# A two-layer hybrid decoder trunk: tiles at multiples of 256 bytes, and layer 1's values and gates projected 512 columns at a time

## The chip, the cores and the metric

The kernel runs on one core of a Trainium2 chip. The metric is the device time of one execution in microseconds (us); the time given for a kernel is the median of its runs. The engines are named as the profile names them: PE is the tensor engine, which multiplies a stationary operand (loaded as "weights", PEld) with a moving one; DVE the vector engine, ACT the scalar engine, POOL the third elementwise engine, SP the engine that issues the DMAs. SBUF is the on-chip memory that operands are read from, PSUM the one that matmuls write to.

## What is computed

Two residual layers on x (512 tokens by 1024 features, float32) and a final norm:

```python
def even_layer(x, g_norm, w_in, b_f, w_out):          # layer 0
    z = rms_norm(x, g_norm) @ w_in                    # q, k, v, gate of 16 + 16 heads of 64, forget gates
    ya = forgetting_attention(hA(qa), hA(ka), hA(va), log_f)   # causal softmax, cumulative log-forget bias
    yb = dilated_attention(hB(qb), hB(kb), hB(vb))             # causal softmax over dilated windows
    return x + concat(ya * silu(ga), yb * silu(gb)) @ w_out

def odd_layer(x, g_norm, w_in, w_out):                # layer 1
    q, k, v, g = split(rms_norm(x, g_norm) @ w_in)    # 4 heads: q, k 256 wide, v, g 512 wide
    y = retention(rotate(q), rotate(k) / 16, v)       # o_t = sum_{s<=t} gamma^(t-s) (q_t.k_s) v_s
    return x + (head_group_norm(y) * silu(g)) @ w_out

out = rms_norm(odd_layer(even_layer(x)), final_norm)
```

## The kernel before

All matmuls of the layers run on `float32r` operands. To keep float32 accuracy, every operand is held as a high and a low part (`split`, L130 to L136: ACT writes the high part, DVE subtracts it for the low part), and a product is three matmuls into the same PSUM tile: high x high, high x low, low x high (`three`, L185 to L188). Thus one line of the page stands for a third of a product.

The normed x is kept transposed in `xT` (128 features of a block, high and low, 8 blocks, 512 tokens). The weights come as a stream of 512 KB chunks: `load_next` issues the DMA of the next chunk of the `plan` into one of three `w_raw` buffers, `split_next` makes its parts `w_h` and `w_l` in one of three buffers each (512 elements of a row at a time, so two ACT and two DVE instructions per chunk) and loads the next; `weights` is called by whoever needs a chunk, so one chunk is split for each one taken.

Three helpers use them. `proj_features` (PSUM tile `pf`) has a chunk of 512 rows by 256 columns as the stationary operand and 512 tokens of `xT` as the moving one: 96 matmuls of 512 columns for 256 features. `proj_tokens` (`pt`) has 128 tokens of `xT` as the stationary operand and 256 columns of a chunk as the moving one: 96 matmuls of 256 columns for 256 features and 512 tokens; two token tiles share a PSUM tile, and the two chunks are used one after the other, each for all four token tiles. `out_proj` (`po`) moves 512 columns of a chunk of 256 rows. PSUM tiles of these three come from one pool of three buffers (`pp`).

Layer 0 works through eight groups of four heads. The projections of the next group and the output projection of an earlier one are fillers, put between the attention steps of a group by `interleave`: logits `ps_s`, softmax on DVE, ACT and POOL, the transposes `ps_pt`, and `ps_o`, probabilities by values. Layer 1 works through four heads in the same way: scores `ps_a` (`kh`, `kl` stationary, `qh`, `ql` moving, 512, 384, 256 and 128 columns wide), retention `ps_r` (`vh`, `vl` moving, 512 wide), group norm on DVE, the gate on POOL, the transposes `ps_yt`. The fillers there are the output projection of the head before and the projections of the next head: `qk`, then the gate (`g_done` copies PSUM to SBUF on DVE; after the last copy ACT applies silu), then the values (`v_done` splits them). Within an engine, instructions run in the order in which the build has put them; an engine that waits holds up all that stands behind.

Tiles are laid out one behind the other in the order in which pools and tiles are made, and small ones take at least 32 bytes of a row. Where they begin in the built program, as the remainder by 256 bytes: `xT` at 128, the weight buffers at 160, layer 0's large tiles (`q`, `k`, `v`, probabilities, `yh`, `yl`) at 64, layer 1's (`kh`, `qh`, `vh`, `ah`, `y1h` and their low parts) and the one extra weight buffer of the last output projection at 32.

## Time and profile before

| | before |
|---|---|
| median of 3 runs | 1035.87 us (1035.27 to 1036.48) |
| span of the profiled execution | 1035.3 us |
| PE busy | 1002.6 us, 97%, 5836 matmuls |
| weight loads (PEld) busy | 869.6 us, 84% |
| DVE busy | 637.0 us, 62% |
| ACT busy | 472.4 us, 46% |
| POOL busy | 247.4 us, 24% |
| HBM read over the span | 85.39 MB, together with writes 85 GB/s |

The profile is one execution, traced on the chip. Busy time counts an instruction from its start to its end; the matmuls of PE are pipelined and overlap, so the busy share says that PE always had one in work, not how fast they follow each other. For that the timeline is read: the distance between the starts of neighbouring matmuls. The chain of work that ended last runs over PE for 81% of the span, over DVE for 7%, DMA for 5% and ACT for 4%.

### The profile page before, as it was taken

Reading aid. Unit: us, or ns where it says so; the run is one execution under the profiler, and the core shown is the slowest. Engines: PE = TensorE matmul, PEld = TensorE weight load, DVE = VectorE, ACT = ScalarE, POOL = GpSimd, SP = SyncE. Lnnn points to the kernel's source line nnn. Section 1 sums busy time; section 2 is a strip of 40 time slices with the busy share of each in tenths; the row PEclk is TensorE's granted clock in tenths of the full one; section 3 lists DMA queues with packets and bytes.
Section 4 is the critical chain, followed back from the end, with each engine's and each line's share of the span. In section 5 each row is a group of like instructions: output and inputs, shape, how many; then the busy total and the mean of one; then the engine's idle time right before and its main releaser. Section 6 shows DMA issues by size and latency. Waiting matters only on the chain.

```text
span 1035.3 us, 15756 instructions
## 1 busy us (share of the span) xinstructions
PE 1002.6 (97%) x5836; PEld 869.6 (84%) x5836; DVE 637.0 (62%) x1389; ACT 472.4 (46%) x987; POOL 247.4 (24%) x326
## 2 busy tenths in 40 slices
PE   5999999999999999999999989999999999999997
PEld 5879788888887888987887769978998899889975
DVE  6465676575584576675657684377645744674476
ACT  5345464464554545644657473333323232333233
POOL 3011354454354352211212140023100300030012
PEclk8999999999999999999999999999999999999999
DMA  7554878635647776437454125321222222312112
GB/s 211 133 134 90 150 100 103 177 77 120 156 90 108 143 84 139 107 79 145 76 130 123 41 62 184 102 79 64 82 82 91 72 82 82 102 61 95 69 41 82
DMA packets 84444, 107.42 MB, mean 104 GB/s; under 512 B 6016, under 2 KB 63616, under 8 KB 84240
## 3 DMA queue, kind: packets, MB, share of 16 engines
q1 hardware_dynamic: 84368, 106.42, 43.4%
q8 instruction: 46, 0.75, 0.3%
q14 instruction: 30, 0.25, 0.1%
HBM read 85.39 MB, written 2.13 MB: 85 GB/s over the span
## 4 chain that ended last, share of the span: by engine, by line
PE 81%; DVE 7%; DMA 5%; ACT 4%; issue 2%; POOL 1%; SPq 0%; DVEq 0%; POOLq 0%; ACTq 0%
PE pf L186 10%; PE pf L187 10%; PE pf L188 10%; PE pt L186 8%; PE pt L188 8%; PE pt L187 8%; PE po L186 5%; PE po L188 5%; PE po L187 5%; PE ps_pt L457 3%; DMA kb<-ka 2%; PE ps_o L470 2%; DVE w_l L134 2%; PE ps_o L469 2%; PE ps_s L443 1%
## 5 line engine op out<-in xcount | busy, mean ns | idle before, releaser
L134 DVE TENSOR_TENSOR w_l<-w_raw,w_h 128x512 fp32r<-128x512 f32 x288 | 218.3, 785 | 95.0 <-ACT w_h L132 81.7
L132 ACT ACTIVATE w_h<-w_raw 128x512 fp32r<-128x512 f32 x288 | 169.5, 627 | 186.0 <-PE pf L187 60.2
L186 PE MATMUL pt<-w_h,xT 128*128 128x256 f32 x768 | 217.1, 283 | 2.2 <-ACT xT L132 2.1
L188 PE MATMUL pt<-w_h,xT 128*128 128x256 f32 x768 | 215.7, 281 | 1.6 <-DVE xT L134 1.6
L187 PE MATMUL pt<-w_l,xT 128*128 128x256 f32 x768 | 215.5, 281 | 0.0
L186 PE MATMUL pf<-xT,w_h 128*128 128x512 f32 x512 | 204.4, 399 | 0.0
L188 PE MATMUL pf<-xT,w_l 128*128 128x512 f32 x512 | 202.9, 396 | 0.0
L187 PE MATMUL pf<-xT,w_h 128*128 128x512 f32 x512 | 202.9, 396 | 0.0
L450 POOL TENSOR_SCALAR pi<-pi,st 128x512 f32<-128x512 f32 (+3 forms) x128 | 73.5, 575 | 377.2 <-DVE st L449 346.6
L186 PEld LDWEIGHTS pt<-w_h,xT 128*128 128x128 f32 x768 | 145.3, 189 | 3.7 <-ACT xT L132 2.9
L188 PEld LDWEIGHTS pt<-w_h,xT 128*128 128x128 f32 x768 | 145.2, 189 | 1.8 <-DVE xT L134 1.8
L187 PEld LDWEIGHTS pt<-w_l,xT 128*128 128x128 f32 x768 | 145.2, 189 | 1.1 <-DVE w_l L134 0.2
L188 PEld LDWEIGHTS pf<-xT,w_l 128*128 128x128 f32 x512 | 96.5, 188 | 23.2
L186 PEld LDWEIGHTS pf<-xT,w_h 128*128 128x128 f32 x512 | 96.7, 189 | 19.9
L187 PEld LDWEIGHTS pf<-xT,w_h 128*128 128x128 f32 x512 | 96.7, 189 | 19.6
L132 ACT ACTIVATE pth<-ps_pt 128x512 fp32r<-128x512 f32 (+3 forms) x128 | 55.3, 432 | 98.2 <-PE ps_pt L457 85.7
L448 ACT ACTIVATE pi<-pi,st 128x512 f32<-128x512 f32 (+3 forms) x128 | 71.4, 558 | 44.4 <-DVE st L446 43.8
L704 POOL TENSOR_TENSOR yn<-yn,gate 128x512 f32<-128x512 f32 x16 | 21.9, 1367 | 262.8 <-DVE yn L703 249.4
L253 DVE TENSOR_TENSOR xres<-po,xres 128x512 f32<-128x512 f32 x88 | 59.6, 683 | 26.6 <-PE po L188 26.1
L134 DVE TENSOR_TENSOR ptl<-ps_pt,pth 128x512 fp32r<-128x512 f32 (+3 forms) x128 | 62.2, 487 | 21.2 <-ACT pth L132 19.4
L457 PE MATMUL ps_pt<-ident,pi 128*128 128x128 f32 x320 | 56.8, 275 | 0.1
L446 DVE CUSTOM_DVE_ANT_0 pi<-ps_s,bias 128x512 f32<-128x512 f32 (+1 forms) x64 | 30.8, 487 | 40.6 <-PE ps_pt L457 20.6
(155 smaller groups left out, 1614.1 us busy)
## 6 DMA issues: line engine op xcount, KB each, us to landing
w_raw<-in_even_w_in_dram SPq DMA_DIRECT2D x64, 512.0 KB, 5.6
w_raw<-in_odd_w_in_dram SPq DMA_DIRECT2D x48, 512.0 KB, 3.5
w_raw<-in_even_w_out_dram SPq DMA_DIRECT2D x16, 512.0 KB, 4.3
w_raw<-in_odd_w_out_dram SPq DMA_DIRECT2D x16, 512.0 KB, 3.5
qb<-qa SPq DMA_DIRECT2D x32, 128.0 KB, 2.9
qb<-qa SPq DMA_DIRECT2D x16, 256.0 KB, 3.2
qa<-qa SPq DMA_DIRECT2D x32, 128.0 KB, 3.1
cs<-c_dram SPq DMA_DIRECT2D x16, 256.0 KB, 3.6
```

The lines of the kernel that those rows point to most:

```text
L132: act.activation(hi, src, AF.Copy, scale=scale)
L134: dve.tensor_tensor(lo, src, r32(hi), ALU.subtract)
L186: pe.matmul(ps, lhsT=ah, rhs=bh, start=first, stop=False)
L187: pe.matmul(ps, lhsT=ah, rhs=bl, start=False, stop=False)
L188: pe.matmul(ps, lhsT=al, rhs=bh, start=False, stop=last)
L253: dve.tensor_tensor(xr, ps, xr, ALU.add)
L446: dve.tensor_tensor_reduce(pi[:, 0:n], ps[:, 0:n], hs["bias"](i), 1.0, 3e38, ALU.add, ALU.min, st[:, 0:1])
L448: act.activation(pi[:, 0:n], pi[:, 0:n], AF.Exp, bias=st[:, 0:1], scale=-1.0, accum_out=st[:, 1:2])
L450: pool.tensor_scalar(pi[:, 0:n], pi[:, 0:n], st[:, 2:3], 1.0, ALU.mult, ALU.mult)
L457: pe.transpose(pt[:, (i - j) * P:(i - j + 1) * P], hs["p"][i][:, j * P:(j + 1) * P], ident)
L469: pe.matmul(po[:, j * P:S], lhsT=v, rhs=th[:, 0:n], start=(j == 0), stop=False)
L704: pool.tensor_tensor(yn, yn, r["g"][:, i, :], ALU.mult)
```

## The change

Two things are changed; comments are gone too, so that line numbers move.

First, padding tiles are put ahead of the large tiles of each pool, the tile `one` takes a whole 256 bytes, and the small tiles of the forget gates, formerly six buffers of the pool `sm`, become slices of one tile. In the built program every tile that a matmul reads begins at a multiple of 256 bytes afterwards; the masks `dil` and `causal`, which only elementwise engines read, don't.

Second, in layer 1 the gates of all heads and the values of all but the first head come from `proj_wide` in place of two `proj_tokens` each. It takes four chunks of 256 rows by 512 columns, and holds them all: the first pass makes token tiles 0 and 1, the second 2 and 3, each with a PSUM tile of 128 tokens by 512 columns of its own. The fourth chunk goes to the extra buffer. Splits for what follows are called in the second pass, when a chunk has been used for the last time. Counted in the built program, 1344 matmuls of 256 columns become 672 of 512. The order of layer 0 stays as it was on every engine.

```diff
+    sm.tile([P, 96], F32, tag="pad", name="pad_sm", bufs=1)
...
+    keep.tile([P, 32], F32, name="pad_keep")
     xres = keep.tile([P, NT, D], F32, name="xres")
...
-    one = keep.tile([P, 1], F32, name="one")
+    one = keep.tile([P, 64], F32, name="one")[:, 0:1]
...
+        cst.tile([P, 56], F32, name="pad_cst")
         dil = cst.tile([P, S], F32, name="dil")
...
+            fg = ap_.tile([P, 8, NT * 16], F32, tag="bias", name="fg", bufs=3)
...
             def tl(n):
-                return sm.tile([P, NT * 16], F32, tag="fgate", name=n, bufs=6)
+                return fg[:, place[n], :]
...
     def weights():
-        split_next()
+
+        if len(ready) < 3:
+            split_next()
+        count["used"] += 1
         return ready.pop(0)
...
+    def proj_wide(w, c0, done):
+
+
+        chunks = [(w[kc * 256:(kc + 1) * 256, c0:c0 + 512], None if kc == 3 else False) for kc in range(4)]
+
+        def work():
+            first, ws = count["used"], []
+            for o in range(2):
+                ps = [pp.tile([P, S], F32, tag="p", name="pw") for _ in range(2)]
+                for kc in range(4):
+                    if o == 0:
+                        if count["split"] < first + 4:
+                            split_next()
+                        count["used"] += 1
+                        ws.append(ready.pop(0))
+                    h, l = ws[kc]
+                    for i in range(2):
+                        t = 2 * o + i
+                        ts_ = slice(t * P, (t + 1) * P)
+                        for k in range(2):
+                            kt = 2 * kc + k
+                            three(ps[i], xT[:, 0, kt, ts_], xT[:, 1, kt, ts_], h[:, k, :], l[:, k, :],
+                                  kt == 0, kt == KT - 1)
+                            if kt == KT - 1:
+                                done(t, ps[i])
+                            yield 3 * MM
+                    if o and (kc < 3 or (loaded and loaded[0][1] is None)):
+                        split_next()
+        return chunks, work(), 96 * MM
...
-        v, g = ([proj_tokens(win1, c0 + 512 * hd + 256 * c, lambda b, ps, r=r, n=n, c=c: late[n](r, c)(b, ps),
-                             by_tile=hd == 0 and n == "v" and c == 0)
-                 for c in range(2)] for n, c0 in (("v", 2048), ("g", 4096)))
+        v, g = ([proj_wide(win1, c0 + 512 * hd, lambda t, ps, r=r, n=n: late[n](r, t, ps))]
+                for n, c0 in (("v", 2048), ("g", 4096)))
+        if hd == 0:
+            v = [proj_tokens(win1, 2048 + 256 * c, lambda b, ps, r=r, c=c: late["v0"](r, c)(b, ps), by_tile=c == 0)
+                 for c in range(2)]
...
+        def v_done(r, t, ps):
+            if t == 0:
+                r["v"] = (hp.tile([P, NT, S], F32R, tag="vh", name="vh"),
+                          hp.tile([P, NT, S], F32R, tag="vl", name="vl"))
+            split(r["v"][0][:, t, :], r["v"][1][:, t, :], ps)
```

PE, in the gate projection of layer 1's second head, before: where the first chunk's work passes from one PSUM tile (`pt0`) to the other; `w_h`, `w_l` are the parts of a chunk, `ps_yt` a transpose of the first head's result.

```order
L712 MATMUL ps_yt_7969<-ident_80,yn_7775 128x128 x4
L186 MATMUL pt0_7852<-w_h_7786,xT_79 128x256
L187 MATMUL pt0_7852<-w_l_7787,xT_79 128x256
L188 MATMUL pt0_7852<-w_h_7786,xT_79 128x256
L186 MATMUL pt1_7853<-w_h_7786,xT_79 128x256
L187 MATMUL pt1_7853<-w_l_7787,xT_79 128x256
L188 MATMUL pt1_7853<-w_h_7786,xT_79 128x256
```

A chunk is used for 24 matmuls on each PSUM tile, then released. After the change, in the same projection, where the first pass ends and the second begins:

```order
L194 MATMUL pw_7590<-w_h_7620,xT_81 128x512
L195 MATMUL pw_7590<-w_l_7621,xT_81 128x512
L196 MATMUL pw_7590<-w_h_7620,xT_81 128x512
L194 MATMUL pw_7701<-w_h_7453,xT_81 128x512
L195 MATMUL pw_7701<-w_l_7454,xT_81 128x512
L196 MATMUL pw_7701<-w_h_7453,xT_81 128x512
```

The matmuls are twice as wide, a chunk serves six on a PSUM tile at a time, and the second pass comes back to the first chunk (`w_h_7453`), which has been held.

ACT, around the values of layer 1's second head, before (`vh` is the evacuation of values, `w_h` the split of a chunk for later work, `gate1` the silu, `y1h` the evacuation of a transpose):

```order
L132 ACTIVATE w_h_8008<-w_raw_7860 128x512 x2
L674 ACT_TABLE_LOAD
L674 ACTIVATE gate1_7818<-gate1_7818 128x2048
L132 ACTIVATE y1h_7717<-ps_yt_8022 128x4x128
L132 ACTIVATE w_h_8071<-w_raw_7946 128x512 x2
L132 ACTIVATE vh_8103<-pt0_8006 128x2x256
L132 ACTIVATE vh_8103<-pt1_8007 128x2x256
L132 ACTIVATE w_h_8135<-w_raw_8014 128x512 x2
L132 ACTIVATE w_h_8191<-w_raw_8077 128x512 x2
L132 ACTIVATE vh_8103<-pt0_8133 128x2x256
L132 ACTIVATE vh_8103<-pt1_8134 128x2x256
L132 ACTIVATE w_h_8264<-w_raw_8141 128x512 x2
```

Splits and evacuations take turns here. After:

```order
L135 ACTIVATE w_h_7815<-w_raw_7771 128x512 x2
L722 ACT_TABLE_LOAD
L722 ACTIVATE gate1_7685<-gate1_7685 128x2048
L135 ACTIVATE y1h_7608<-ps_yt_7828 128x4x128
L135 ACTIVATE vh_7874<-pw_7823 128x512
L135 ACTIVATE vh_7874<-pw_7824 128x512
L135 ACTIVATE w_h_7900<-w_raw_7798 128x512 x2
L135 ACTIVATE w_h_7920<-w_raw_7821 128x512 x2
L135 ACTIVATE w_h_7940<-w_raw_7906 128x512 x2
L135 ACTIVATE vh_7874<-pw_7886 128x512
L135 ACTIVATE vh_7874<-pw_7887 128x512
```

Three splits, of chunks for the next output projection, now stand in a row between the evacuations of the first and of the second pass; the same pairs stand on DVE.

## Rows read from the trace of the kernel before

**Rows 1.** Page, part 1: busy time, share of the span, instructions of each engine.

```profile
PE 1002.6 (97%) x5836; PEld 869.6 (84%) x5836; DVE 637.0 (62%) x1389; ACT 472.4 (46%) x987; POOL 247.4 (24%) x326
```

**Rows 2.** By stretch: us; busy PE, PEld, DVE, ACT, POOL (instructions); clock, DMA, GB/s.

```profile
0.00:24.00 24.00, 12.61 (x72) 11.42 (x73) 16.32 (x30) 12.06 (x25) 8.40 (x9) 0.86 0.72 216
...
60.00:600.00 540.00, 530.92 (x2921) 450.55 (x2920) 347.68 (x848) 291.85 (x659) 178.28 (x273) 1.00 0.56 112
600.00:620.00 20.00, 16.73 (x92) 14.26 (x91) 16.25 (x37) 15.43 (x36) 10.23 (x8) 0.91 0.18 54
620.00:1010.00 390.00, 388.34 (x2482) 349.52 (x2481) 224.94 (x406) 130.23 (x220) 44.03 (x31) 1.00 0.26 86
1010.00:1036.00 26.00, 18.04 (x82) 14.34 (x81) 15.37 (x41) 9.88 (x24) 6.43 (x5) 0.95 0.22 81
```

**Rows 3.** Waits of PE: total us, times, longest; the first of eighteen lines.

```profile
PE ps_xt L143 <- DVE xT L134: 5.0, 2, 3.6
```

**Rows 4.** Groups by line and shape, PE: count, busy us, mean ns, idle before.

```profile
L186 PE MATMUL pt<-w_h,xT 128*128 128x256 f32 x768 | 217.1, 283 | 2.2 <-ACT xT L132 2.1
...
L186 PE MATMUL pf<-xT,w_h 128*128 128x512 f32 x512 | 204.4, 399 | 0.0
...
L186 PE MATMUL po<-w_h,yh 128*128 128x512 f32 x128 | 51.6, 403 | 1.8 <-DVE v L134 0.9 <-DVE xres L253 0.5 <-ACT yh L132 0.4
```

**Rows 5.** Timeline of PE, layer 1's first head: start us, duration us.

```profile
664.16 0.40 PE L186 MATMUL pf<-xT,w_h 128*128 128x512 f32 x1
...
673.96 0.40 PE L186 MATMUL pf<-xT,w_h 128*128 128x512 f32 x1
```

**Rows 6.** Timeline of PE, token projections of the same head.

```profile
640.01 0.28 PE L186 MATMUL pt<-w_h,xT 128*128 128x256 f32 x1
...
646.31 0.28 PE L186 MATMUL pt<-w_h,xT 128*128 128x256 f32 x1
```

**Rows 7.** Timeline of PE, output projection in layer 1.

```profile
767.67 0.40 PE L188 MATMUL po<-w_h,y1l 128*128 128x512 f32 x1
...
770.93 0.40 PE L187 MATMUL po<-w_l,y1h 128*128 128x512 f32 x1
```

**Rows 8.** Timeline of PE, six scores of 512 columns and what follows.

```profile
969.85 0.39 PE L186 MATMUL ps_a<-qh,kh 128*128 128x512 f32 x1
...
971.21 0.40 PE L186 MATMUL po<-w_h,y1h 128*128 128x512 f32 x1
```

**Rows 9.** Timeline of PE, three scores of 384 columns and what follows.

```profile
773.33 0.33 PE L186 MATMUL ps_a<-qh,kh 128*128 128x384 f32 x1
...
773.85 0.40 PE L186 MATMUL po<-w_h,y1h 128*128 128x512 f32 x1
```

**Rows 10.** Timeline of PE, six scores of 256 columns and what follows.

```profile
778.75 0.28 PE L186 MATMUL ps_a<-qh,kh 128*128 128x256 f32 x1
...
779.47 0.39 PE L186 MATMUL po<-w_h,y1h 128*128 128x512 f32 x1
```

**Rows 11.** Timeline of PE, nine retention matmuls of the last head.

```profile
1006.41 0.39 PE L186 MATMUL ps_r<-vh,ah 128*128 128x512 f32 x1
...
1008.45 0.40 PE L186 MATMUL po<-w_h,y1h 128*128 128x512 f32 x1
```

**Rows 12.** Timeline of PE, five scores of 128 columns and what follows.

```profile
785.11 0.27 PE L187 MATMUL ps_a<-ql,kh 128*128 128x128 f32 x1
...
785.67 0.45 PE L186 MATMUL po<-w_h,y1h 128*128 128x512 f32 x1
```

**Rows 13.** Groups by line and shape, ACT and DVE: splits and evacuations of values.

```profile
L132 ACT ACTIVATE w_h<-w_raw 128x512 fp32r<-128x512 f32 x288 | 169.5, 627 | 186.0 <-PE pf L187 60.2 <-PE pt L188 51.7 <-issue 32.4
...
L132 ACT ACTIVATE vh<-pt 128x512 fp32r<-128x512 f32 x16 | 9.6, 598 | 27.0 <-PE pt L188 27.0
...
L134 DVE TENSOR_TENSOR vl<-pt,vh 128x512 fp32r<-128x512 f32 x16 | 11.1, 691 | 25.0 <-ACT vh L132 24.9
```

More of the change, by code (lines that the diff above doesn't have):

```diff
@@ L149, in trunk @@
     plan, loaded, ready, late = [], [], [], {}
+    count = dict(split=0, used=0)
     def load_next():
@@ L176, in split_next @@
             ready.append((h, l))
+            count["split"] += 1
         load_next()
     def weights():
-        split_next()
+        if len(ready) < 3:
+            split_next()
+        count["used"] += 1
         return ready.pop(0)
@@ L341, in forget_gates @@
                 pe.transpose(zt[:, t, :], z[:, t * P:(t + 1) * P], ident[0:32, 0:32])
+            fg = ap_.tile([P, 8, NT * 16], F32, tag="bias", name="fg", bufs=3)
+            place = dict(f_z=0, f_nz=1, f_mz=2, f_na=3, f_e=4, f_den=5, f_rec=6, f_s=7, f_s2=0, f_pol=1, f_lf=3)
             def tl(n):
-                return sm.tile([P, NT * 16], F32, tag="fgate", name=n, bufs=6)
+                return fg[:, place[n], :]
             zz = tl("f_z")
@@ L656, in rotate_done, with v0_done @@
             return done
-        def v_done(r, c):
+        def v0_done(r, c):
             def done(b, ps):
@@ L665, in v_done, with g_done @@
             return done
-        def g_done(r, c):
-            def done(b, ps):
-                if b == 0 and c == 0:
-                    r["g"] = hp.tile([P, NT, S], F32, tag="gate1", name="gate1", bufs=2)
-                cs = slice(256 * c, 256 * (c + 1))
-                dve.tensor_copy(r["g"][:, 2 * b:2 * b + 2, cs], ps)
-                if b == 1 and c == 1:
-                    act.activation(r["g"], r["g"], AF.Silu)
-            return done
+        def v_done(r, t, ps):
[3 more added lines that the diff above has]
+            split(r["v"][0][:, t, :], r["v"][1][:, t, :], ps)
+        def g_done(r, t, ps):
+            if t == 0:
+                r["g"] = hp.tile([P, NT, S], F32, tag="gate1", name="gate1", bufs=2)
+            dve.tensor_copy(r["g"][:, t, :], ps)
+            if t == NT - 1:
+                act.activation(r["g"], r["g"], AF.Silu)
         def scores(r, j):
@@ L720, in trunk @@
         REST = [(retain, 0), (retain, 1), (y_block, 0), (retain, 2), (y_block, 1), (retain, 3), (y_block, 2), (y_block, 3)]
-        late.update(wpool=l1.enter_context(tc.tile_pool(name="wlast", bufs=1)), rotate=rotate_done, v=v_done, g=g_done)
+        late.update(wpool=l1.enter_context(tc.tile_pool(name="wlast", bufs=1)), rotate=rotate_done,
+                    v0=v0_done, v=v_done, g=g_done)
         for f in R[0]["proj"]:
```

## The prediction

> **What bounds the kernel now.** I read the page's busy shares first: the tensor engine (PE) is busy 97% of 1035.3 us, the vector engine (DVE) 62% [rows 1]. A share over the whole span hides stages, so the second view is the busy time by stretch [rows 2]: in layer 0 PE works 530.92 of 540 us, in layer 1 388.34 of 390, in the first 24 us only 12.61 and in the last 26 only 18.04. The third is PE's list of waits; its longest entry is 5.0 us in total [rows 3]. PE hardly waits, so the time can only fall if PE's instructions follow each other faster, or become fewer.
>
> The page's mean durations (399 ns for a 512-column matmul, 283 for a 256-column one [rows 4]) are no measure of that, because matmuls overlap. What counts is the pitch, the distance from one start to the next, read from the timeline. In the K and Q projections `pf`, 42 matmuls go by between the two rows of [rows 5]: 9.80 us, so 233.3 ns each. In the token projections `pt`, 54 between those of [rows 6]: 6.30 us, so 116.7 ns. In the output projections `po`, 14 between the outer rows of [rows 7]: 3.26 us, so 232.9 ns. In these stretches the granted clock is 1.00 [rows 2], the upper level of 2.4 GHz.
>
> Is 233 ns what 512 columns cost? The score matmuls `ps_a` answer, since they have three widths and one kind of operand: six of 512 columns take 1.36 us, 226.7 ns each [rows 8]; three of 384 take 0.52, 173.3 each [rows 9]; six of 256 take 0.72, 120.0 each [rows 10]. From 256 to 512 columns that is 106.7 ns, or 0.417 ns a column, one column per cycle. So 512 columns are worth 213.3 ns, and something fixed is added to each matmul: 13.3 ns in `ps_a` at every width, 20 in `pf` and `po`, 10 in `pt`. **This extra depends on which operands are used**, not on the width alone. And where tiles start differs in just this way: layer 1's own tiles, which `ps_a` reads for both operands, lie 32 bytes past a multiple of 256; in `pf` the operands lie at 128 and 160, in `po` at 160 and at 32 or 64, in `pt` at 160 and 128. No row has an operand at 0. The retention matmuls, both operands at 32 too, run nine in a row at 2.04 us, again 226.7 each [rows 11].
>
> **The change, part by part.** *Alignment.* The padding puts every large tile that a matmul reads at a multiple of 256 bytes; in layer 0 no instruction moves for it. It acts on the extra of each matmul. Bounds: at best the extra vanishes, 213.3 ns; the best pitch that any row shows for this width is 226.7; if starts don't matter, 233.3 stays; below nothing, see the third rival. I take 216, an estimate near the floor: the operands at 32 bytes show the smallest extra at 512 columns, and of all starts in the trace 32 is nearest to 0. That is a choice, and the weakest step here.
>
> The Trainium skill, "TensorE: Matmul & The Clock Gate", "Back-to-back issue gap", gives N / 2.4 + 2.5 ns, thus 216 ns for 512 columns. The rows disagree by 17 ns; by that figure as an estimate the sum would be the same as mine.
>
> Terms, with the counts of [rows 4] (`pf` three lines of 512; `po` six of 128; `pt` three of 768):
> - `pf`: 1536 x (233.3 - 216) = 26.6 us.
> - `po`: 768 x (232.9 - 216) = 13.0 us.
> - the other 288 matmuls of 512 columns (retention 120, scores 24, attention 128, forget gates 16): from 226.7 to 216, 3.1 us.
> - 152 of 384 and 152 of 256 columns in attention and scores: 173.3 to 162.7 and 120 to 112, 2.8 us.
>
> *256-column matmuls that stay.* 768 in layer 0 and 192 in layer 1's first value. Below about 112 ns they can't go: matmuls of 128 columns, each with a weight load of its own, have 0.56 / 5 = 112 ns [rows 12], so that is the pace of weight loads. 960 x (116.7 - 112) = 4.5 us.
>
> *The wide projections.* Seven pairs of token projections (gates of four heads, values of three) become seven wide ones: 1344 matmuls of 256 columns become 672 of 512. Same columns, half the matmuls and weight loads: 1344 x 116.7 = 156.8 us, against 672 x 216 = 145.2, a gain of 11.6 us. Without the alignment it would be 672 x 233.3 = 156.8: nothing. So this half lives off the other one.
>
> What it moves: a wide one holds four chunks through two passes, so the splits for what follows can only start in its second pass, three in a row on ACT ahead of the last two evacuations, where they had been spread. I cost it at nothing. The third split waits for chunk 2, released 12 matmuls (2.6 us) before the pass ends; its two ACT halves take 2 x 0.627 us [rows 13], and the first evacuation behind it becomes due after 6 matmuls, 1.3 us. The PSUM buffer of that tile is next wanted 24 matmuls later, 5 us. The tight place is between the passes: with three buffers, the second pass' second tile takes the buffer of the first pass' first, 12 matmuls, 2.6 us, after its last matmul, and evacuating takes 0.598 + 0.691 us [rows 13]. Cover 1.3 us. If it were gone every time, 7 x 1.3 = 9 us. Splits per column stay the same, the loads stay at 512 KB, and PE shows no wait for a load of weights.
>
> *Forget gates in one tile.* The same small DVE operations once; nothing.
>
> Sum: 26.6 + 13.0 + 3.1 + 2.8 + 4.5 + 11.6 = 61.6 us of PE pitch. Not all arrives. At the start, at the turn of the layers and at the end PE waits for others [rows 2], and some 250 of 5836 matmuls lie there: 2 us lost. In layer 0 PE is idle 9 us between 60 and 600 us; when PE is 6% faster, DVE (347.68 of those 540 us [rows 2]) and ACT are not, so I add 3 us of new waits, a third of that idle time. Net 56.6 us. The profiled execution's span is 1035.3 us and the median of the runs 1035.87, so 0.6 lies around it: 1035.9 - 56.6 = **979 us**. With 213.3 in place of 216 the 3264 wide matmuls give 9 us more, and with 256-column matmuls at 109 another 3: 967 us; 962 if no gain is lost either.
>
> **The rivals.**
> 1. *Part of it.* A common start is what helps, not zero: all pitches become those of [rows 8] and [rows 11], 226.7. `pf` 10.1 us, `po` 4.8, wide 4.5, and the 256-column ones lose 3.2, since [rows 10] has 120 where `pt` has 116.7. Net 16 to 18, so 1018 us. For it: it takes nothing that no row shows. Against: it leaves the 13 ns unexplained, and a start of 32 is not one of 0.
> 2. *The change doesn't do what it says*: the extra belongs to the operand type or to the tiles, not to starts. Then 233.3 stays, the wide part gives nothing, 1036 us. For it: `pf` and `po`, with quite different starts, show the same 20 ns within 1 ns. Against: [rows 8] and [rows 5] differ by 6.6 ns at one width and one clock.
> 3. *Slower.* With everything at 0, the reads of the moving operand and of the next matmul's weights would step through SBUF alike and get in each other's way. [rows 10] shows such a case, both at 32: 120.0 against the 116.7 of [rows 6], 2.9% more. On the streaming time, 2304 x 233.3 + 156.8 + 960 x 116.7 ns = 806 us, that is +23: 1059 us. It decides once the pitch of 512 columns passes 233.3. Against: the same common start is the fastest at 512.
>
> The Trainium skill, the same page, "Step-by-step: what each phase is for", holds that loading the next weights takes no read bandwidth from the running matmul, which has a read port of its own. By that rule the third rival can't happen; no run here shows it yet, but [rows 10] lean the other way.
>
> **How the numbers follow.** Forecast (965 to 995): 0.60, because the fixed extra varies with the operands and the floor is known, but the value at 0 is not seen. First rival (995 to 1027): 0.18. Second (1034 to 1038): 0.11. Third, with the lost cover of the wide part: 0.11. A measurement of this kernel can tell 0.2%, 2 us, from no change. Faster by more: 0.60 + 0.18 = 0.78; within: 0.11; slower: 0.11. The range reaches from just under the floor without loss, 960, to the end of the first rival's likely times, 1020, and leaves out 0.22.
>
> **What would show it.** In the profile after: the pitch of `pf` and `po` near 216 ns (226 says the first rival, 233 the second, 237 or more the third); `pt` near 112 and the wide tiles at the pitch of `pf`; 5164 matmuls for 5836; PE in layer 1 still busy without a gap, or else waits of the wide tiles for a split or an evacuation; more PE idle time in layer 0 than 9 us. The forecast is wrong if the pitch stays, or if it falls and waits in layer 0 take more than 10 us back.

## The result, and the profile after

The changed kernel takes 1028.32 us (median of four runs, 1027.94 to 1028.93), beside 1035.97 us (1035.27 to 1036.48) for the kernel before in the same rounds. The ratio is 0.9921, with a 95% interval of 0.9908 to 0.9933: 0.8% faster, 7.6 us, where 57 were forecast. Two later groups of runs gave 1028.45 and 1028.44 us, ratios 0.9924 [0.9913, 0.9936] and 0.9915 [0.9902, 0.9929]. The profiled executions' spans are 1026.3 and, before, 1035.3 us.

The page of the changed kernel, part 1 (busy time, share of the span, instructions), answers to [rows 1]:

```profile
PE 990.4 (96%) x5164; PEld 839.8 (82%) x5164; DVE 634.8 (62%) x1389; ACT 472.8 (46%) x987; POOL 244.8 (24%) x326
```

The busy time by stretch answers to [rows 2] (columns as there):

```profile
0.00:24.00 24.00, 12.48 (x66) 11.43 (x67) 14.77 (x28) 11.39 (x23) 8.57 (x9) 0.79 0.70 216
...
60.00:600.00 540.00, 530.21 (x2939) 454.17 (x2938) 351.47 (x855) 295.24 (x666) 179.08 (x276) 1.00 0.55 113
600.00:620.00 20.00, 16.65 (x108) 15.04 (x107) 15.18 (x35) 14.69 (x34) 7.16 (x6) 0.91 0.15 38
620.00:1010.00 390.00, 385.92 (x1818) 321.82 (x1817) 228.52 (x417) 132.57 (x226) 47.43 (x34) 1.00 0.27 86
```

PE is as full as before, between 60 and 600 us idle for 9.8 us against 9.1. The wide projections save their 672 matmuls (5164 for 5836), but in those 540 us of layer 0 hardly more instructions pass than before: 2939 against 2921. So the pitch has to be read, in the same places. The first two rows below are the K and Q projections of layer 1's first head (timeline of PE: start us, duration us), as in [rows 5], the second two the token projections before them, as in [rows 6]:

```profile
658.00 0.39 PE L194 MATMUL pf<-xT,w_h 128*128 128x512 f32 x1
...
681.58 0.39 PE L196 MATMUL pf<-xT,w_l 128*128 128x512 f32 x1
```

```profile
627.22 0.28 PE L194 MATMUL pt<-w_h,xT 128*128 128x256 f32 x1
...
636.10 0.28 PE L196 MATMUL pt<-w_h,xT 128*128 128x256 f32 x1
```

Between the first two go 104 matmuls in 23.58 us: 226.7 ns each, down from 233.3. Between the second two go 74 in 8.88 us: 120.0 ns, **up** from 116.7. These are the two figures of the operands at 32, [rows 8] and [rows 10], and not the 216 and 112 of the forecast. In layer 0, where a projection's matmuls stand in short pieces, even 226.7 does not hold. Between two attention steps it looks like this:

```profile
166.15 0.33 PE L514 MATMUL ps_o<-ptl,v 128*128 128x384 f32 x1
166.32 0.39 PE L194 MATMUL pf<-xT,w_h 128*128 128x512 f32 x1
166.55 0.40 PE L195 MATMUL pf<-xT,w_h 128*128 128x512 f32 x1
166.78 0.40 PE L196 MATMUL pf<-xT,w_l 128*128 128x512 f32 x1
167.02 0.39 PE L194 MATMUL pf<-xT,w_h 128*128 128x512 f32 x1
167.25 0.39 PE L195 MATMUL pf<-xT,w_h 128*128 128x512 f32 x1
167.48 0.40 PE L196 MATMUL pf<-xT,w_l 128*128 128x512 f32 x1
167.71 0.39 PE L194 MATMUL pf<-xT,w_h 128*128 128x512 f32 x1
167.94 0.40 PE L195 MATMUL pf<-xT,w_h 128*128 128x512 f32 x1
168.17 0.39 PE L196 MATMUL pf<-xT,w_l 128*128 128x512 f32 x1
168.40 0.39 PE L194 MATMUL pf<-xT,w_h 128*128 128x512 f32 x1
...
169.54 0.39 PE L196 MATMUL pf<-xT,w_l 128*128 128x512 f32 x1
```

The first nine steps, 166.32 to 168.40, take 2.08 us, 231 ns each; the five from there to 169.54 take 1.14, 227 by the unrounded starts. Over all of layer 0 `pf` has 229.5 ns, where it had 232.9 before.

PE's waits, to be held against [rows 3] (total us, times, longest):

```profile
PE pt L194 <- ACT xT L135: 4.2, 1, 4.2
PE ps_xt L146 <- DVE xT L137: 3.1, 2, 2.9
PE ps_o L514 <- DVE ptl L137: 2.9, 2, 2.2
PE warm L633 <- DMA ident<-in_ident_dram: 2.7, 1, 2.7
PE ps_r L194 <- DVE yn L750: 2.5, 2, 2.2
```

Two are larger than before, here and in both repeats of the changed kernel. The first `pt` waits 4.2 us (3.2 and 3.6 in the repeats), where it waited 2.1. And a retention in layer 1 waits 2.2 us for the group norm of the one before, which it did not.

In both repeats this second wait costs more than itself, for the granted clock falls behind it. By stretch (columns as in [rows 2]), first the profile above, then one of the repeats:

```profile
710.00:714.00 4.00, 3.41 (x15) 2.77 (x16) 3.96 (x8) 0.00 (x0) 1.29 (x1) 1.00 0.33 118
710.00:714.00 4.00, 3.61 (x9) 2.89 (x10) 2.95 (x6) 0.00 (x0) 1.27 (x1) 0.57 0.35 116
```

In the repeat the retention's matmuls follow each other every 0.43 us in place of 0.23, part of the stretch being at the lower level of 1.2 GHz; layer 1 as a whole is 1.1 to 1.3 us longer in the repeats.

To see where the time went, each stretch from one start on PE to the next is put to the tile of the first of the two; so waits, and stretches at a lower clock, are in the sums. Layer 0 is counted up to the last transpose of layer 1's x, so its `pt` holds the first 58 token projections of layer 1 as well. Worked out from the traces of before, of the change's two halves alone (below) and of after, one execution each, in us:

| PE, from start to start | before | wide alone | aligned alone | after |
|---|---|---|---|---|
| layer 0: `pf` | 273.1 | 272.8 | 269.9 | 268.7 |
| layer 0: `po` | 96.5 | 96.5 | 95.2 | 96.6 |
| layer 0: `pt` | 108.5 | 107.1 | 110.1 | 109.5 |
| transposes of x, both layers, `ps_xt` | 10.1 | 11.9 | 9.5 | 11.9 |
| layer 0: attention, rest | 133.1 | 131.6 | 131.8 | 130.7 |
| **layer 0** | 621.3 | 619.9 | 616.5 | 617.4 |
| layer 1: `pf` | 91.4 | 91.4 | 89.3 | 89.3 |
| layer 1: `po` | 89.7 | 89.4 | 88.1 | 88.2 |
| layer 1: values, gates (`pt`, `pw`) | 173.3 | 175.2 | 178.0 | 172.1 |
| layer 1: rest | 49.3 | 49.5 | 49.3 | 49.1 |
| **layer 1** | 403.7 | 405.5 | 404.7 | 398.7 |

Repeats of the changed kernel gave 615.1 and 617.2 for layer 0, 400.0 and 399.8 for layer 1; a single entry is good to about 1.5 us (`po` in layer 0, 96.6 here, has 95.1 in both repeats).

### The profile page after: what moved, and what is told of

It reads as the page before. It is cut to its first block, busy times and chain, and to the rows that moved or that the text cites. A ratio compares the mean times of both kernels' runs of the same rounds, so it can differ in the third digit from the quotient of the medians.

```text
span 1026.3 us, 14404 instructions
## 1 busy us (share of the span) xinstructions
PE 990.4 (96%) x5164; PEld 839.8 (82%) x5164; DVE 634.8 (62%) x1389; ACT 472.8 (46%) x987; POOL 244.8 (24%) x326
## 4 chain that ended last, share of the span: by engine, by line
PE 80%; DVE 8%; DMA 5%; ACT 4%; issue 2%; POOL 1%; SPq 0%; DVEq 0%; POOLq 0%; ACTq 0%
PE pf L194 10%; PE pf L195 10%; PE pf L196 10%; PE pw L196 5%; PE pw L194 5%; PE pw L195 5%; PE po L194 4%; PE po L196 4%; PE po L195 4%; PE ps_pt L501 3%; PE pt L196 3%; PE pt L194 3%; PE pt L195 3%; DVE w_l L137 2%; PE ps_o L514 2%
## 5 line engine op out<-in xcount | busy, mean ns | idle before, releaser
L137 DVE TENSOR_TENSOR w_l<-w_raw,w_h 128x512 fp32r<-128x512 f32 x288 | 215.2, 774 | 104.1 <-ACT w_h L135 88.5
L194 PE MATMUL pf<-xT,w_h 128*128 128x512 f32 x512 | 201.5, 394 | 0.0
L196 PE MATMUL pf<-xT,w_l 128*128 128x512 f32 x512 | 200.5, 392 | 0.0
L195 PE MATMUL pf<-xT,w_h 128*128 128x512 f32 x512 | 200.3, 391 | 0.0
L194 PE MATMUL pt<-w_h,xT 128*128 128x256 f32 x320 | 92.7, 290 | 4.3 <-ACT xT L135 4.2
L196 PE MATMUL pt<-w_h,xT 128*128 128x256 f32 x320 | 92.0, 288 | 1.6 <-DVE xT L137 1.6
L195 PE MATMUL pt<-w_l,xT 128*128 128x256 f32 x320 | 92.0, 287 | 0.0
L194 PE MATMUL pw<-w_h,xT 128*128 128x512 f32 x224 | 88.1, 393 | 0.0
L196 PE MATMUL pw<-w_h,xT 128*128 128x512 f32 x224 | 87.3, 390 | 0.0
L195 PE MATMUL pw<-w_l,xT 128*128 128x512 f32 x224 | 87.2, 389 | 0.0
L194 PEld LDWEIGHTS pt<-w_h,xT 128*128 128x128 f32 x320 | 62.4, 195 | 5.6 <-ACT xT L135 5.0
L196 PEld LDWEIGHTS pt<-w_h,xT 128*128 128x128 f32 x320 | 62.3, 195 | 1.8 <-DVE xT L137 1.8
```

What stands on the lines that cost most here:

```text
L137: dve.tensor_tensor(lo, src, r32(hi), ALU.subtract)
L194: pe.matmul(ps, lhsT=ah, rhs=bh, start=first, stop=False)
L195: pe.matmul(ps, lhsT=ah, rhs=bl, start=False, stop=False)
L196: pe.matmul(ps, lhsT=al, rhs=bh, start=False, stop=last)
```

## The experiments

The theories: **A**, the common start counts, whatever it is; **B**, a start of 0 is special; **C**, the wide projections bring the gain by themselves; **D**, the rest of the extra comes from loading the stationary operand; later **E**, a stream of 512-column matmuls loses its pitch at every break and needs some matmuls to find it again, and **F**, the higher pitch in layer 0 comes from DVE and ACT working beside PE.

### The two halves apart

Alignment alone: the padding as in the change, values and gates of layer 1 as before.

```diff
-        v, g = ([proj_wide(win1, c0 + 512 * hd, lambda t, ps, r=r, n=n: late[n](r, t, ps))]
-                for n, c0 in (("v", 2048), ("g", 4096)))
...
+        v, g = ([proj_tokens(win1, c0 + 512 * hd + 256 * c, lambda b, ps, r=r, n=n, c=c: late[n](r, c)(b, ps),
+                             by_tile=hd == 0 and n == "v" and c == 0)
+                 for c in range(2)] for n, c0 in (("v", 2048), ("g", 4096)))
...
```

> The changed kernel with the wide projections undone: layer 1's gates and values come from 256-column token projections again, all tiles stay at multiples of 256 bytes. Theory A (a common start of moving and stationary operand lets a stream of matmuls settle at 226.7 ns for 512 columns and at 120 for 256): pf and po gain 4.3 ns on each of 2304 matmuls, 9.9 us, pt loses 2.7 ns on each of 2304, 6.2 us; about 1032 us. Theory B (the start at 0 itself does it): the same. Theory C (the wide form alone brings the gain, starts do nothing): pitch 233, 1036 us.

Measured: 1033.06 us, ratio 0.9964 [0.9950, 0.9978], span 1031.4: what A and B say, C is 3 us off.

Wide alone: the change without its padding, so with the starts of before.

```diff
-    sm.tile([P, 96], F32, tag="pad", name="pad_sm", bufs=1)
...
-    keep.tile([P, 32], F32, name="pad_keep")
...
-    one = keep.tile([P, 64], F32, name="one")[:, 0:1]
+    one = keep.tile([P, 1], F32, name="one")
...
-        cst.tile([P, 56], F32, name="pad_cst")
```

> The changed kernel without the padding tiles, so that tiles start where they did before (xT 128, weights 160, layer 0's tiles 64, layer 1's 32 bytes past a multiple of 256), with the wide projections. Theories A and B: the wide tiles have 233 ns like pf, 672 x 233.3 = 156.8 us against 156.8 before, so 1036 us within 2. Theory C: 1028 us.

Measured: 1039.88 us, ratio 1.0027 [1.0014, 1.0041], span 1035.7. So C is out: alone, the wide half is 0.3% slower. The profiled execution, at 1037.49 us, is one of the faster of ten (1036.86 to 1041.56), so the table doesn't hold the whole of that loss. It does say why the two halves need each other. Alignment takes 5.3 us off `pf` and 2.9 off `po`, but gives 4.7 back in layer 1's 256-column matmuls (173.3 to 178.0) and 1.6 in layer 0's. The wide projections alone change the pitch by nothing (their 672 matmuls run at 233.2 ns, the 1344 before at 116.7 to 117.2) and cost waits (the first `pt` 4.2 us, the retention 2.0). Together, the wide half turns just those 256-column matmuls that alignment slows down into 512-column ones that it speeds up: 178.0 to 172.1.

### All tiles at 32

Every tile that a matmul reads begins 32 bytes past a multiple of 256.

```diff
-    keep.tile([P, 32], F32, name="pad_keep")
+    keep.tile([P, 40], F32, name="pad_keep")
```

> The changed kernel with 32 bytes more of padding at the front: every tile that a matmul reads starts 32 bytes past a multiple of 256, all alike. Theory A (a common start): the same as the change, 1028 us, pf at 227 to 229 ns. Theory B (a start at 0): pf back at 233 ns and the time at 1036 us.

Measured: 1031.14 us, ratio 0.9952 [0.9935, 0.9969], span 1027.8. Long runs of `pf` again have 226.7 ns, `pt` 120, the wide tiles 227.2, layer 0's `pf` 229.4: pitch by pitch the changed kernel. B is out. That the median is 2.8 us above the changed kernel's, with a span only 1.5 above, no pitch explains; it stays open.

### A scan of starts

Only streams: 36 matmuls in a row on 128 x 128 stationary operands, each stream with its own pair of starts, all multiples of 32 from 0 (a) to 224 (h).

```diff
+    for i, mo in enumerate(AT):
+        for j, so in enumerate(AT):
+            stream("w" + L[i] + L[j] + "_", mo, so, 512, 36)
+    for i, mo in enumerate(AT):
+        for j, so in enumerate(AT):
+            stream("n" + L[i] + L[j] + "_", mo, so, 256, 36)
```

> No layer is computed (x is copied to the output): streams of 36 matmuls each from SBUF tiles that start at a multiple of 256 bytes, with the moving operand at one of 8 offsets (0 to 224 bytes in steps of 32; first letter a to h) and the stationary one at one of 8 (second letter), at 512 columns (names w) and 256 (names n); then 512 columns with 64 and 32 stationary columns (names x and y). Theory A: 226.7 ns where both letters are the same, about 233 elsewhere, and 120 against 116.7 at 256 columns. Theory B: 226.7 only at aa. A third, D (the extra belongs to the weight load that goes with each matmul): fewer stationary columns bring the pitch nearer to 213.3; by A they change nothing.

Timeline of PE, each row one stream (start us, duration, and the count at the end; w is 512 columns, n is 256, the first letter the start of the moving operand, the second of the stationary one):

```profile
27.48 8.33 PE L45 MATMUL waa__137<-mv,st 128*128 128x512 f32 x36
35.64 8.55 PE L45 MATMUL wab__175<-mv,st 128*128 128x512 f32 x36
44.03 8.33 PE L45 MATMUL wac__213<-mv,st 128*128 128x512 f32 x35
```

```profile
561.79 4.47 PE L45 MATMUL naa__2569<-mv,st 128*128 128x256 f32 x36
566.10 4.42 PE L45 MATMUL nab__2607<-mv,st 128*128 128x256 f32 x36
570.36 4.41 PE L45 MATMUL nac__2645<-mv,st 128*128 128x256 f32 x36
```

From start to start, equal starts take 8.16 us for 36, 32 bytes apart 8.39. With the first twelve of each stream left out, the pitch of all 64 pairs at 512 columns goes by the difference alone, moving minus stationary, modulo 256; at 256 columns some differences have two values (ns):

| difference | 0 | 32 | 64 | 96 | 128 | 160 | 192 | 224 |
|---|---|---|---|---|---|---|---|---|
| 512 columns | 226.7 | 233.3 | 228.8 | 233.2 | 232.7 | 234.1 | 233.4 | 233.4 |
| 256 columns | 120.0 | 116.7 to 117.9 | 117.8 | 119.8 to 120.2 | 118.7 | 117.2 to 120.0 | 113.3 to 117.8 | 118.3 |

That is theory A in a sharper form: a difference of 64 is nearly as good as none. It reads the rows of before too: in [rows 5] and [rows 6] `xT` begins at 128 and the weights at 160, a difference of 224 for `pf` and of 32 for `pt`, and in [rows 7] the difference is 128 (232.9 ns there, 232.7 here). Equal starts are the best for 512 columns and about the worst for 256. No pair comes below 226.7. Streams with 64 or 32 stationary columns, at six pairs of starts, have 229 to 240 ns, not less, so D is not borne out.

### Breaks, and another operand type

Streams of 512 columns at equal starts (fe) and 32 bytes apart (fd), broken after every 3, 6, 12 or 24 by one matmul of 128 columns, or by four float32 transposes; then bfloat16 operands (b).

```diff
+                for r in range(96 // every):
+                    if kind == "f":
+                        pe.matmul(tw[:, 0:128], lhsT=st[:, 0:128], rhs=mv[:, 0:128], start=True, stop=True)
...
+                    for k in range(every):
...
+                        pe.matmul(ps, lhsT=st[:, b:b + P], rhs=mv[:, a:a + 512], start=kk == 0, stop=kk == 95)
...
+            pe.matmul(ps, lhsT=bs[:, b:b + P], rhs=bm[:, a:a + 512], start=k == 0, stop=k == 35)
```

> Only streams of matmuls into PSUM, no work of the two layers, DVE and ACT idle beside them; the output is the input. Streams at equal starts are broken after every 3, 6, 12 or 24 matmuls of 512 columns by one matmul of 128 columns or by four float32 transposes. Theory E (a break costs the lock, and the stream needs some nine matmuls to find back to 226.7 ns): within pieces of 12 the mean pitch is 229 to 231 ns as in the changed kernel between attention steps, within pieces of 24 about 228, in pieces of 3 and 6 above 230; the first nine pitches after a break repeat a pattern from 224 to 236 ns. Theory F (the 228.8 ns of the changed kernel come from DVE and ACT working beside PE): the broken streams stay at 226.7 ns whatever their length, since nothing else works here. 256 columns, starts 64 bytes apart, longer streams: if 113.3 ns is a steady state, most of these go to 113.3; if it was a chance of the short streams, 117 to 118. 384 columns: 173.3 ns at equal starts, up to 180 otherwise. bfloat16, 512 columns: if the fixed extra belongs to float32r, 213 to 216 ns whatever the starts; if it belongs to every matmul, 226.7 at equal starts and 233 otherwise. One stationary operand for all matmuls: the same pitch as before if the operand is loaded each time anyway.

Timeline of PE, the pieces of 24 at the place where equal starts give way to starts 32 bytes apart (t is the break), and the first two bfloat16 streams, at equal starts and 32 bytes apart:

```profile
518.76 5.68 PE L82 MATMUL fe__3066<-mv,st 128*128 128x512 f32 x24
524.28 0.22 PE L74 MATMUL t<-mv,st 128*128 128x128 f32 x1
524.34 5.81 PE L82 MATMUL fd__3168<-mv,st 128*128 128x512 f32 x24
529.99 0.22 PE L74 MATMUL t<-mv,st 128*128 128x128 f32 x1
...
594.96 7.94 PE L91 MATMUL baa__3498<-bm,bs 128*128 128x512 bf16 x35
602.74 7.93 PE L91 MATMUL bab__3536<-bm,bs 128*128 128x512 bf16 x35
610.51 7.93 PE L91 MATMUL bca__3574<-bm,bs 128*128 128x512 bf16 x35
```

A piece of 24 takes 5.52 us at equal starts and 5.65 at others. Mean steps within a piece, in ns, after a 128-column break, the first one (which has the break's own cost) left out:

| piece | equal starts | 32 bytes apart |
|---|---|---|
| 3 | 236 | 229 |
| 6 | 231.9 | 231.0 |
| 12 | 229.2 | 233.0 |
| 24 | 227.8 | 233.1 |

At equal starts the steps of three of the four pieces of 24 go 284, 231, 236, 228, 233, 231 and from there 227 or 226, and the fourth gets there one step sooner: the pitch has to be found again after each break. Behind a matmul of 128 columns nothing is gained in pieces of 6 or fewer. After transposes it takes six or ten steps, and pieces of 6 have 231.3 ns against 233.2. No other engine works beside these streams, so breaks alone can raise the mean pitch to that of layer 0's pieces, as E says, and F isn't needed.

Not every change is such a break. In the changed kernel `pf` behind the retention, whose matmuls have 512 columns as well, is at 227 from its first step (five pieces of five); its nine steps here take 2.04 us, 226.7 each, where the nine of layer 0 above had 231:

```profile
701.66 0.39 PE L196 MATMUL ps_r<-vh,al 128*128 128x512 f32 x1
701.89 0.39 PE L194 MATMUL pf<-xT,w_h 128*128 128x512 f32 x1
...
703.93 0.39 PE L194 MATMUL pf<-xT,w_h 128*128 128x512 f32 x1
```

Behind scores of 384 or 256 columns `po` and `pf` need five steps or more. And in the scan, of the seven streams of 512 columns at equal starts that follow one with another difference, six have 226 to 227 from their first step. So it is narrower matmuls and transposes that break a stream; another pair of starts mostly doesn't.

The bfloat16 streams follow each other every 7.77 to 7.78 us, 36 matmuls each (in some a record is missing): 216 ns, whatever their starts. So **the extra beyond 216 belongs to `float32r`** (of the two types tried), and its size to the starts and to what was running before. One stationary operand for all matmuls gave 226.7 and 233.4 once more. The 256-column streams, 96 long, with starts 64 bytes apart either way settle at 117.8 in all eight cases; the 113.3 that three short streams had did not come again here.

### Longer pieces in the kernel itself

In layer 0, projection work only after every second attention step, twice as much at a time.

```diff
             step()
+            if not upto and i % 2 == 0 and i < n - 1:
+                continue
```

> The changed kernel, but in layer 0 projection work is put in only after every second attention step, twice as much at a time; in the built program some of it still moves between the steps. Theory E (a stream of 512 columns needs about nine matmuls after each break to reach 226.7 ns): the mean pitch of layer 0's pf falls from 229.5 ns towards 228, that of po from 230 to about 229: 1152 x 1 + 384 x 1 ns, 1 to 2 us of pitch. What the attention steps, now two in a row, wait for DVE, ACT and POOL comes on top: 1 to 10 us more waiting, so 1027 to 1037 as a whole. Theory F (the higher pitch of layer 0 comes from DVE and ACT working beside PE): the pitch of pf stays at 229.5 ns.

Measured: 1059.37 us, ratio 1.0210 [1.0196, 1.0224]. The pitch does what E says: layer 0's `pf` falls from 229.5 to 228.6 ns, `po` from 230 to 229.0, and by the length of the pieces the traces give, over both layers (ns, steps counted in brackets; a step of more than 250 ns ends a piece):

| length of a piece of `pf` | before | after | longer pieces |
|---|---|---|---|
| 7 to 11 | 232.7 (117) | 230.5 (117) | 230.4 (218) |
| 12 to 15 | 233.0 (730) | 229.6 (744) | 228.5 (131) |
| 16 to 23 | 233.0 (151) | 227.9 (151) | 228.1 (327) |
| 24 to 47 | 233.3 (72) | 226.7 (72) | 227.7 (414) |
| 48 and more | 233.3 (199) | 226.8 (199) | 226.8 (199) |

But layer 0 as a whole takes 646.6 us against 617.4, far more than the 1 to 10 us expected: the attention steps that now stand two in a row wait for what the other engines make between them. PE's idle time grows from 9.8 us (60 to 600 us) to 21.2 (60 to 630 us); the rest stands in longer steps, which the overlap of PE's matmuls hides in its busy time: where `ps_o` stands right behind `pf`, 28 of 32 steps take over 300 ns, and the changed kernel has one such place. Some 1 us of pitch cost 29 us. The short pieces are the price of the cover, and worth it.

### Starts 64 bytes apart in layer 0

By the scan, with `xT` 64 bytes past the weights, `pf` would have 228.8 ns, which layer 0 doesn't better anyway, and `pt` up to 6 ns less. Every use of `xT` becomes `xTs[0]`.

```diff
-    xT = keep.tile([P, 2, KT, S], F32R, name="xT")
+    xall = keep.tile([P, 2 * KT * S + 64], F32R, name="xT")
+    # x^T begins 64 bytes past a multiple of 256 in layer 0, at a multiple of 256 in layer 1
+    xTs = [xall[:, o:o + 2 * KT * S].rearrange("p (a k s) -> p a k s", a=2, k=KT) for o in (16, 0)]
...
             if t == 0 and c == 0:
+                del xTs[0]
```

> The changed kernel with the transposed x 64 bytes past a multiple of 256 in layer 0 alone; all else begins at a multiple of 256, and nothing moves. By the scan's table (only the difference of the two starts counts, also between attention steps) the 1152 matmuls of 512 columns in layer 0's projections have moving minus stationary = 64, thus 228.8 ns and no change against their present 228.8 to 229; the 768 of 256 columns have 192, thus 113.3 to 117.8 ns in place of 119.7: 1.5 to 4.9 us faster than the changed kernel, 1023.5 to 1027. Rival (in streams between attention steps 64 apart is not better than any other difference, 233 ns): 1152 x 4.3 = 5.0 us back, less 1.5 to 4.9: 1028 to 1032.

> The changed kernel once more, on the chip and in the rounds of the other run, as the measure for it: 1028 +- 1 us. In its first profile, and in those of the two other kernels with wide projections, the first chunk of weights reached SBUF 1.9 us later than before (the first pt at 13.9 us, not 12.0), with the same order on the queue. If this belongs to the program, the first pt is again at 13.5 to 14.2 us; if it was the chance of single executions, it may be anywhere from 12.0.

Measured: 1027.51 us, ratio 0.9912 [0.9899, 0.9925], beside 1028.45 for the changed kernel. Once more, in other rounds:

> The changed kernel with the transposed x at 64 in layer 0, once more, beside the changed kernel in the same rounds. If the shorter pitch of layer 0's 256-column matmuls arrives: 1 to 2.5 us below the other. If it goes into waits: within 0.5 us of it.

> The changed kernel, as the measure for the two other runs: 1028 +- 1 us, the first pt at 13.5 to 14.2 us again.

Measured: 1028.43 us, ratio 0.9914 [0.9899, 0.9928], beside 1028.44. The pitch came: layer 0's `pt` take 106.2 us in both runs, against 109.5, 109.0 and 109.2 (steps of 113.3 as well as of 117.7 stand in it). The time didn't: in the mean `pf` takes 0.6 us more, `po` 0.6, the attention's logits, transposes and products 1.4, and layer 0 as a whole comes to 617.5 and 614.6 us, within the spread of the changed kernel's 617.4, 615.1 and 617.2. No version found beats the changed kernel by more than can be measured.

### The two new waits

At the start, the first transposed x is split ahead of the first chunk; in layer 1, more projection work is put between a head's first two retentions.

```diff
                 if t == 1:
+                    transpose_tile(0, xn[0])
                     split_next()
                 dve.tensor_scalar(xn[t], xn[t], r, None, ALU.mult)
-                transpose_tile(t - 1, xn[t - 1])
+                if t > 1:
+                    transpose_tile(t - 1, xn[t - 1])
...
-        UPTO = (.06, .12, .18, .24, .30, .36, .42, .48, .55, .62, .68, .74)
+        UPTO = (.06, .12, .18, .24, .35, .38, .42, .48, .55, .62, .68, .74)
```

> The changed kernel with two of its new waits taken away: at the start the first transposed x is split before the first chunk of weights, which arrives later in it than before the change; and in layer 1 more projection work stands between the first and the second retention of a head, whose PSUM buffer is held up by splits of chunks on DVE. If these two waits (4.2 us before the first pt, of which 2.1 are new, and 2.2 us at the second retention of the first head) lie on the path and nothing takes their place: the first pt at 13.2 us or earlier, no ps_r wait over 0.5 us, the whole 1 to 4 us faster than the changed kernel's 1028.4: 1024 to 1027. If the work at the start is bounded by the arrival of the transfers, only the 2.2 us of the retention come: 1026. If both only move on to the next wait: 1028.

> The same with the transposed x 64 bytes past a multiple of 256 in layer 0. By the pitches of the earlier run with that start (pt of layer 0 about 117 ns against 121 to 122, pf 0.4 ns more) layer 0's projections take 2.5 us less, so 1.5 to 2.5 us below the other run of this pair. In that earlier run only 0.9 us came of it, with an uncertainty of 1.3. If the gain goes into waits of layer 0 for DVE and ACT, the two are equal within 1 us.

Measured: 1034.94 us, ratio 0.9981 [0.9967, 0.9995], and with `xT` at 64 in layer 0 1032.15, ratio 0.9967 [0.9954, 0.9980]: both slower than the changed kernel with its ratios of 0.9915 to 0.9924. The second is 2.8 us below the first, more than either expectation; beside the changed kernel the same start brought 0.9 and 0.0 us, so nothing is built on it. PE's waits in the first of them:

```profile
PE pt L194 <- ACT w_h L135: 4.4, 2, 3.2
PE ps_r L194 <- DVE yn L752: 3.9, 2, 2.8
```

The first `pt` does start earlier, at 13.06 us for 13.85, but the first `pf` comes at 34.86 against 34.23: the start is bounded by the chunks that arrive, and the wait has only moved on to the next split. The retention's wait grew. Why, the changed kernel's DVE shows (timeline of DVE around the place where PE waits until 710.59):

```profile
704.69 0.69 DVE L137 TENSOR_TENSOR w_l<-w_raw,w_h 128x512 fp32r<-128x512 f32 x1 [2.31 <-ACT w_h L135]
705.30 0.69 DVE L744 BATCH_NORM_STATS2 bn<-ps_r 128x6 f32<-128x512 f32 x1
705.91 0.68 DVE L137 TENSOR_TENSOR w_l<-w_raw,w_h 128x512 fp32r<-128x512 f32 x1
...
709.72 0.81 DVE L750 TENSOR_SCALAR yn<-ps_r,mv,rs 128x512 f32<-128x512 f32 x1
```

The first retention's matmuls had begun at 701.21, but its norm starts only at 705.30, for it stands on DVE behind the split of a chunk, which waits 2.31 us for ACT and that for the chunk's arrival (ACT's `w_h` begins at 704.02). The splits of two chunks in a row, there for the wide projection, stand around and in the norm; `yn` frees the only PSUM buffer of `ps_r` at 710.5. Before, the norm began 1.0 us after its retention (706.08 on PE):

```profile
707.10 0.69 DVE L697 BATCH_NORM_STATS2 bn<-ps_r 128x6 f32<-128x512 f32 x1
```

More work on PE in between doesn't shorten that. This is read from the order on DVE; no run takes the splits away from there. The spans of the two profiles, 1029.1 and 1028.8 us, lie 2 to 4 us above the changed kernel's 1025.2 to 1027.3; the median of the first is 6.5 us above (its executions scatter from 1031 to 1037). Part of that can be the clock: it averages 0.988 over its twelve executions and 0.991 over the changed kernel's fourteen, an estimate of 3 us at most for 1030 us; what the rest is stays open.

## Why the prediction was wrong, and where it was right

**What bounds the kernel: right.** PE's pitch is the time. From before to after the table loses 8.9 us; the two spans differ by 9.0.

**That the extra goes by the operands' starts: right. The step that failed is the choice of 216 ns for a start of 0**, the one that the prediction called its weakest. It took 32 to be near to 0 and read a trend into a single point. [Rows 8 to 11] have both operands at one start, the rows of `pf`, `pt` and `po` at two; the scan shows that only the difference counts, and that 32 is as good as 0. The first rival said so, with the right figures (226.7 and 120), and got 0.18; with them the sum of 61.6 us is 16.2. What stood against it, that it leaves 13 ns unexplained, was no argument: 216 is what bfloat16 takes, and none of the 64 pairs of starts gives it to `float32r`. So the second rival (the extra belongs to the operand type) had a part of the truth: 10.7 of the 17 ns over 216.

Term by term, predicted against measured (us, from the table above, waits included in the measured ones; in the two repeats `po` has 3.1, the wide projections 0.3 and 1.6):

| term | forecast | first rival | measured |
|---|---|---|---|
| `pf` | 26.6 | 10.1 | 6.5 |
| `po` | 13.0 | 4.8 | 1.4 |
| wide projections | 11.6 | 4.5 | 1.6 |
| 256-column matmuls that stay | 4.5 | -3.2 | -1.4 |
| attention, retention, other | 5.9 | | 2.6 |
| start and new waits | -5 | | -1.8 |

The 256-column matmuls had the wrong sign. The pace of weight loads, 112 ns [rows 12], was taken as the value they would reach; no stream of 256 columns came below 113.3, and [rows 10] showed 120 for a common start.

**The first rival's 1018 us was too low as well**, by 10 us, and this is what the runs added. It took 226.7 everywhere. But of the 1026 steps of `pf` in layer 0 that stand in pieces of three or more, 730 are in pieces of 12 to 15 and 201 in shorter ones, where a piece is over soon after it has found its pitch: 229.6 to 230.5. By the mean pitches of `pf`, `po` and the wide tiles this comes to 5.7 us as an estimate, 4.6 of them in layer 0; the waits at the retention (2.2) and at the start (1.8) make most of the rest. The trace of before could hardly show that: at unequal starts pieces of every length have 233, and [rows 8], six matmuls at 226.7 right behind 256-column ones, even spoke against it; why these need no steps to find their pitch is not settled.

**Without the alignment the wide half gives nothing: right**, and sharper than said: alone it costs 0.3%, and alignment alone gives 6.3 of the 8.2 us back that it takes off `pf` and `po`. **The wide splits at no cost: nearly.** The place named as tight, the PSUM buffer between the passes, shows no wait. It cost 2.2 us at another: the retention's norm, which the splits stand in front of, and in both repeats a stretch at the lower clock on top. The start lost 1.8 us, near the 2 allowed for it but for another reason: not gain that doesn't arrive, but a first chunk that is split at 12.2 us where it had been at 10.3. Layer 0 gained no waits, since it hardly became faster.

**The third rival** did not come at 512 columns. The Trainium skill, "TensorE: Matmul & The Clock Gate", "Step-by-step: what each phase is for", by which the weight load takes no read bandwidth from the running matmul, agrees with that. Why the stationary operand's start counts at all, that rule doesn't tell, and no run here separates the load from the stream. The Trainium skill, the same page, "Back-to-back issue gap", gives N / 2.4 + 2.5 ns, 216 for 512 columns; the bfloat16 streams agree with it, the operand type of this kernel does not.

## What to carry to other kernels

Before a floor is put into a sum, find it in a row of the same operand type; where two classes of rows differ, ask what all of one class share before drawing a line through one of them. With `float32r` operands, give both operands of 512-column matmuls the same start modulo 256 bytes, and check what that does to narrower ones: here alignment alone brought 0.4%, widening alone lost 0.3%, both together won 0.8%. A pitch measured in a long stream isn't that of pieces of a dozen between narrower matmuls, and longer pieces may cost far more in waits than they give back in pitch.

## What the runs showed of the hardware that was not expected

- `float32r`, 512 columns, at 1.00 of the clock: 226.7 ns at equal starts modulo 256 bytes, 228.8 with the moving operand 64 bytes further, 232.7 to 234.1 at all other multiples of 32. 384 columns: 173.3 at three pairs, 176.6 at the fourth, with a difference of 192. 256 columns: 120.0 at equal starts, 113.3 to 120.2 elsewhere. 128 columns: 111.6 to 111.7 at the four pairs tried. bfloat16, 512 columns: 216 at all five pairs.
- After a break the 226.7 is found again only after 5 or 6 steps (a 128-column matmul), or 6 to 10 (transposes); behind a 512-column matmul at another pair of starts it was there from the first step in six streams of seven.
- Executions of one kernel differ in the granted clock behind the same wait: after the 2.2 us at the retention it was 1.00 in one profile of the changed kernel (710 to 714 us) and 0.57 and 0.63 in the two repeats.
- The first chunk of weights is split at 12.1 to 12.4 us in every profile of a program with wide projections (ten of them), and at 10.3 in both without, though the first dozen DMAs stand in the same order on SP's queue. Moving the waiting work didn't win it back; where it comes from was not settled.
